# One core of a hybrid decoder step: the sample's attention steps stand still while the prompt's attention outputs are merged

## The chip, the cores and the metric

The kernel runs on one core of a Trainium2 chip. The metric is the device time of one launch in microseconds (us): the median of three runs before the change is 1683.92 us (1680.46 to 1686.54). TensorE is called PE, VectorE DVE, ScalarE ACT, GpSimd POOL, and SyncE, which issues most transfers, SP.

## The reference, cut to what matters

One layer of a decoder for 1024 prompt tokens and 32 sample tokens (8 sequences of 4). All arithmetic is float32.

```
h = rmsnorm(x) * (1 + sc1) + sh1
q, k, v, u_lin, u_gate, gate_a, gate_b = split(h @ w_in)
a = conv_tail(depthwise(u_lin * sigmoid(u_gate))) @ w_conv_out
for three groups of 4 heads (windows 128, 512, 2048, dilations 1, 4, 16):
    prompt: o, lse = dilated attention over the group's own keys
    sample: o, lse = attention over the cached keys and values and the 4 new ones
o = sum over groups of softmax(lse over groups) * o        # the merge
b = o @ w_attn_out
x = x + g1 * ((sigmoid(gate_a) * a + sigmoid(gate_b) * b) @ w_out)
x = x + g2 * moe(rmsnorm(x) ...)     # top 2 of 32 experts, then the outputs
```

## The kernel before

The order of the work is written out by hand: each engine has one queue, and instructions stand in it in the order in which the program emits them. An engine that waits for one instruction holds up all that stand behind it.

**Pieces.** The product `h @ w_in` is made in pieces of 128 columns (`run_piece`, line 1089; list `pieces`). There are 50: for each of six head pairs q, k and v (and for the first four pairs two pieces of the convolution's input, ul and ug), numbers 0 to 25; then the gates, ga c and gb c, and from the third pair of gates on a piece ab c that multiplies the convolution's and the attention's outputs by w_conv_out and w_attn_out. So 26 to 31 are ga0, gb0, ga1, gb1, ga2, gb2; 32 is ab0; 33 and 34 are ga3 and gb3; 35 is ab1; then ga4, gb4, ab2, ga5, gb5, ab3 and so on to 49. A piece has three column parts of 352 tokens. Numbers are split into a high and a low part, so that each product is three matmuls: a gate piece has 3 x 8 x 3 = 72 of them, an ab piece 3 x (12 + 6) = 54. A gate piece is evacuated by ACT (tanh, line 1141), out of three PSUM buffers; an ab piece by DVE (lines 1114 to 1121). The weights of the next piece are split while a piece runs: the high part by ACT (line 171), the low part (line 172) by POOL for pieces up to 33 and by DVE from 34 on.

**Modulation.** From piece 34 on, two units of the second modulation product run in each piece (`run_mb`, line 1060): a load of 512 KB, a split by ACT and DVE (tiles mbh, mbl), four matmuls.

**Ticks.** Everything else is written as generators that are advanced a step at a time by `tick()` (line 1183). A piece has 9 ticks, the first one 3, so that piece j holds ticks 9j - 5 to 9j + 3. One tick advances the attention generators (`att_bg`) by one step; the convolution (`conv_bg`) in two ticks of three; and the low-priority generators (`low_bg`) in two ticks of three, those whose number leaves 0 or 2 when divided by 3.

**The merge.** `att_bg` runs the prompt's attention of the six head pairs and then `merge_gen` (line 861). Each of eight row blocks is loaded from a DRAM buffer (og, line 869) that the attention wrote; DVE and, for one exponential, ACT (line 834) merge the groups (`merge_steps`, lines 824 to 854), two blocks at a time; PE transposes the result (line 895), ACT and DVE split it into oTh and oTl (lines 898, 900), and the block two pairs later is loaded. The generator starts at tick 247. It has 42 steps and would end at tick 288, but piece 31 ends with tick 282, and ahead of piece 32 (ab0), the first reader of oTh and oTl, the program drains `att_bg` (line 1261): the last six steps are emitted there with no ticks between them.

**The sample's attention.** `low_bg` runs `sample_logits` for each head group and then `sample_out` (line 970): a first step (the new rows' output, the first load, the maximum and the exponentials), which falls on tick 246; a second with three products of the new values (tile pt_vx, line 984), on tick 248; then 20 chunks of cached values, two steps each. A chunk is four loads of 128 KB by SP (line 927, issued one chunk ahead), one multiply by POOL over 128 x 1024 elements (line 999), one reduction (line 1001) and one addition (line 1002) by DVE. Chunk k (1 to 20) is reduced at tick 249 + 3k. Behind the chunks come a trip through DRAM, a small merge and one transpose, step 56 being the last, at tick 329 (piece 37).

All large tiles come from one pool of 44 slots. A load into a slot waits for the last reader of what the slot held.

Behind the pieces come the product with w_out and the router (`p4_mm` and its neighbours), then the experts, whose weights are streamed from HBM, then the outputs.

Of the kernel before, what the change touches and what calls it, by code (L numbers as in the profile page):

```python
# [72 lines left out]
def nrow(i):  # L73
    return NS if i == SI else P
# [66 lines left out]
def hybrid(ctx, tc, A, O):  # L141
# [12 lines left out]
    def slot(shape, name, dtype=F32):  # L154
        return slots.tile(shape, dtype, name=name, tag="s", bufs=NSLOT)
# [4 lines left out]
    def ptr(shape, name):  # L160
        return ps.tile(shape, F32, name=name, tag="T", bufs=2)
# [4 lines left out]
    def f(ap):  # L166
        return ap.bitcast(F32)
# [319 lines left out]
    def mm3(out, wpair, ks, xs, cols, tick=None):  # L487

        hi, lo = wpair
        n = len(ks)  # L490
        for a, (k, (xh, xl)) in enumerate(zip(ks, xs)):
            pe.matmul(out, hi[:, k], xh[:, cols], start=a == 0, stop=False)  # L492
            pe.matmul(out, lo[:, k], xh[:, cols], start=False, stop=False)  # L493
            pe.matmul(out, hi[:, k], xl[:, cols], start=False, stop=a == n - 1)  # L494
            if tick and a in (2, 5):
                tick()
# [25 lines left out]
    conv_bg, att_bg, low_bg = Bg(), Bg(), Bg()  # L522
# [301 lines left out]
    def merge_steps(n, nparts, src, o):  # L824

        v = src.rearrange("p (g h) x -> p g h x", h=4)
        nm = ep.tile([P, 4], F32, name="mg_nm", tag="mg_nm", bufs=2)
        dve.tensor_reduce(nm[:n], v[:, :, :, 64].rearrange("p g h -> p h g"), axis=AX.X, op=ALU.min)
        yield
        w = ep.tile([P, 4, 4], F32, name="mg_w", tag="mg_w", bufs=2)  # L830
        wv = w[:n, 0:nparts]
        dve.tensor_tensor(wv, nm[:n, None, :].to_broadcast([n, nparts, 4]), v[:, :, :, 64], op=ALU.subtract)
        yield
        act.activation(wv, wv, AF.Exp)
        yield
        ws = ep.tile([P, 4, 4], F32, name="mg_ws", tag="mg_ws", bufs=2)
        dve.tensor_tensor(ws[:n, 0:nparts], wv, v[:, :, :, 65], op=ALU.mult)
        yield
        den = ep.tile([P, 4], F32, name="mg_d", tag="mg_d", bufs=2)
        dve.tensor_reduce(den[:n], ws[:n, 0:nparts].rearrange("p g h -> p h g"), axis=AX.X, op=ALU.add)  # L840
        yield
        dve.reciprocal(den[:n], den[:n])
        yield
        dve.tensor_tensor(wv, wv, den[:n, None, :].to_broadcast([n, nparts, 4]), op=ALU.mult)
        yield
        o = o.rearrange("p (h d) -> p h d", h=4)
        tm = v[:, :, :, 0:64]
        dve.tensor_tensor(tm, tm, wv[:, :, :, None].to_broadcast([n, nparts, 4, HD]), op=ALU.mult)
        yield
        dve.tensor_tensor(o[:n], tm[:, 0], tm[:, 1], op=ALU.add)  # L850
        yield
        for gg in range(2, nparts):
            dve.tensor_tensor(o[:n], o[:n], tm[:, gg], op=ALU.add)
            yield
# [6 lines left out]
    def merge_gen():  # L861
        for c in range(2):
            oT.append((slot([P, S], f"oTh{c}", F32R), slot([P, S], f"oTl{c}", F32R)))
        tt, o = {}, {}

        def load(i):
            if i < 8:
                tt[i] = slot([P, SLOT], f"mg{i}")
                sp.dma_start(tt[i][:, 0:792], og[i * P:(i + 1) * P].rearrange("p a x -> p (a x)"))

        load(0)
        load(1)
        for _ in range(8):
            yield
        for i in range(0, 10, 2):
            ms = []
            for k in (i, i + 1):
                if k < 8:
                    t = tt[k]
                    ms.append(merge_steps(P, 3, t[:, 0:792].rearrange("p (a x) -> p a x", x=66), t[:, 792:1048]))  # L880
            for _ in zip(*ms):
                pass
            if not i:
                load(2)
                load(3)
            yield
            yield
            yield
            yield
            for k in (i - 2, i - 1):  # L890
                if k >= 0:
                    q = tt.pop(k)[:, 792:1048]
                    pt = ptr([P, 2, P], f"pt_o{k}")
                    for c in range(2):
                        pe.transpose(pt[:, c], q[:, c * P:(c + 1) * P], ident)
                    cs = slice(k * P, (k + 1) * P)
                    for c in range(2):
                        act.activation(oT[c][0][:, cs], pt[:, c], AF.Copy)
                    for c in range(2):
                        dve.tensor_tensor(oT[c][1][:, cs], pt[:, c], f(oT[c][0][:, cs]), op=ALU.subtract)  # L900
                    load(k + 4)
                    yield
            yield


    oTs = cp.tile([P, 2, NS], F32, name="oTs")
# [113 lines left out]
    def copy_gen():  # L1020
        for g in range(3):
            keep = (124, 508, 1024)[g]
            drop = CACHE[g] - keep
            n = keep * 512
            m = n // (1, 2, 4)[g]
            for b in range(DB):
                for o in range(0, n, m):
                    sp.dma_start(dap(kvs[g], b * (keep + 4) * 512 + o, [[m // 16, 16], [1, m // 16]]),
                                  dap(caches[g], (b * CACHE[g] + drop) * 512 + o, [[m // 16, 16], [1, m // 16]]))
                    yield  # L1030
        sp.dma_start(conv_s[0, :, 0:26].rearrange("b r c -> b (r c)"),
                       A["state_conv"][0, :, 4:30].rearrange("b r c -> b (r c)"))
        yield
# [55 lines left out]
    def run_piece(j):  # L1089
# [19 lines left out]
        for n in range(3):  # L1109
# [20 lines left out]
            else:  # L1130
                if j == 0:
                    pm = pms[n]
                else:
                    pm = pmm([P, NTILE], f"pm_{j}_{n}")
                    mm3(pm, W[j], range(KC), hT, cs, tick)
# [25 lines left out]
            for _ in range(3 if kind == "ab" else 1):  # L1161
                tick()
        W[j] = None
        if kind == "ul":
            lin[c] = dst
        elif kind == "ug":
            lin.pop(c)
            conv_bg.add(conv_gen(c))
            if c == 3:
                conv_bg.add(conv_tail())  # L1170
        elif kind in ("q", "k", "v"):
            qk.setdefault(c, {})[kind] = dst
            if kind == "v":
                att_bg.add(pair_gen(c))
                if c == 5:
                    att_bg.add(merge_gen())
# [1 line left out]
    setup = [dw_T, state_T] + [lambda p=p: bias_rows(p) for p in range(6)] + [early_t.clear]  # L1178
    copies, wo_bg = Bg(), Bg()
    copies.add(copy_gen())  # L1180
    state = {"n": 0}

    def tick():
        n = state["n"] = state["n"] + 1
        if n % 3 == 0:
            if setup:
                setup.pop(0)()
            if n > 45:
                copies.step(1, 1)
        att_bg.step(1, 1)  # L1190
        if n % 3 or CR:
            conv_bg.step(1, 1)
        if n % 3 != 1:
            low_bg.step(1, 1)
            wo_bg.step(1, 1)

    for j in range(2):
# [626 lines left out]
    with tc.If(vmax > P + HB):  # L1824
# [25 lines left out]
        for i in range(9):  # L1850
            n = nrow(i)
# [151 lines left out]
```

## Time and profile before

| | us |
|---|---|
| median of three runs | 1683.92 |
| profiled execution, its own time | 1680.3 |
| span of the profiled execution | 1678.5 |
| mean granted PE clock over the span | 0.956 |
| pieces 26 to 31, from the sample's second step (579.65) to ab0 (651.62) | 72.0 |
| ab0 (651.62) to the start of ga3 (664.69) | 13.1 |
| ga3 to the start of ab1 (689.95) | 25.3 |
| ab1 to the start of ga5 (743.02) | 53.1 |

Times within the span are counted from its first instruction. The stretches by piece begin at the piece's first matmul on PE. A row of windows gives for each engine the time in which it was busy and the number of its instructions, then the granted clock of PE (1.00 is full speed), the share of the DMA engines and GB/s. In a row of a group of instructions the mean duration of one and its number are what is wanted; in a row of waits the total, the number of times and the longest.

### The profile page before, as it was taken

Reading aid. Unit: us, or ns where it says so; the run is one execution under the profiler, and the core shown is the slowest. Engines: PE = TensorE matmul, PEld = TensorE weight load, DVE = VectorE, ACT = ScalarE, POOL = GpSimd, SP = SyncE. Lnnn points to the kernel's source line nnn. Section 1 sums busy time; section 2 is a strip of 40 time slices with the busy share of each in tenths; the row PEclk is TensorE's granted clock in tenths of the full one; section 3 lists DMA queues with packets and bytes.
Section 4 is the critical chain, followed back from the end, with each engine's and each line's share of the span. In section 5 each row is a group of like instructions: output and inputs, shape, how many; then the busy total and the mean of one; then the engine's idle time right before and its main releaser. Section 6 shows DMA issues by size and latency. Waiting matters only on the chain. (4 is left out here: it accounts for less than half of the span.)

```text
span 1678.5 us, 22927 instructions
## 1 busy us (share of the span) xinstructions
PE 1523.2 (91%) x8238; PEld 1067.2 (64%) x8238; DVE 868.1 (52%) x1502; ACT 457.8 (27%) x938; POOL 466.0 (28%) x403
## 2 busy tenths in 40 slices
PE   5999989999799887999989996999999999999991
PEld 3789978998789776899977875433333333333330
DVE  5684878777933689844465466222222222222224
ACT  7523332333244411233333321111111111111113
POOL 2111143113411454300003434222242333332330
PEclk9899998999999988999999996799999999999996
DMA  9132365354442564744467329878799999999996
GB/s 327 53 108 84 133 191 189 104 187 124 140 121 63 135 169 127 201 134 149 128 226 220 126 72 361 312 237 310 259 383 387 397 382 386 373 394 387 383 345 218
DMA packets 202030, 378.73 MB, mean 226 GB/s; under 512 B 33981, under 2 KB 121193, under 8 KB 200976
## 3 DMA queue, kind: packets, MB, share of 16 engines
q1 hardware_dynamic: 183095, 346.79, 59.0%
q0 software_dynamic: 18784, 29.99, 6.8%
q8 instruction: 88, 1.44, 0.3%
q14 instruction: 63, 0.51, 0.1%
HBM read 358.00 MB, written 66.93 MB: 253 GB/s over the span
## 5 line engine op out<-in xcount | busy, mean ns | idle before, releaser
L492 PE MATMUL pm<-hTh,wh 128*128 128x352 f32 x984 | 340.7, 346 | 3.0 <-ACT wh L171 3.0
L493 PE MATMUL pm<-hTh,wl 128*128 128x352 f32 x984 | 324.8, 330 | 8.3 <-POOL wl L172 8.3
L494 PE MATMUL pm<-hTl,wh 128*128 128x352 f32 x984 | 323.3, 329 | 0.0
L1675 PE MATMUL gu<-raw,x0s 128*64 128x512 f32 x1024 | 237.9, 602 | 14.0 <-PEq L1803 4.8
L492 PEld LDWEIGHTS pm<-hTh,wh 128*128 128x128 f32 x984 | 190.1, 193 | 15.3 <-issue 4.4
L493 PEld LDWEIGHTS pm<-hTh,wl 128*128 128x128 f32 x984 | 190.5, 194 | 13.0 <-POOL wl L172 11.6
L172 POOL TENSOR_TENSOR wl<-wr,wh 128x1024 fp32r<-128x1024 f32 (+1 forms) x34 | 84.4, 2482 | 381.5 <-ACT wh L171 286.1
L494 PEld LDWEIGHTS pm<-hTl,wh 128*128 128x128 f32 x984 | 190.2, 193 | 0.0
L1675 PE MATMUL py<-raw,xhs 128*64 128x512 f32 x768 | 174.0, 592 | 0.5 <-ACT xhs L1696 0.5
L1675 PEld LDWEIGHTS gu<-raw,x0s 128*64 128x64 f32 x1024 | 74.9, 137 | 151.3 <-issue 141.4
L557 DVE SCALAR_TENSOR_TENSOR acc<-u,dwT,acc 128x1024 f32<-128x1024 f32 x120 | 169.8, 1415 | 0.0
L1690 DVE SCALAR_TENSOR_TENSOR hu<-hu,gu 64x512 f32<-64x512 f32 x48 | 32.6, 679 | 257.6 <-ACT hu L1689 122.4
L1675 PEld LDWEIGHTS py<-raw,xhs 128*64 128x64 f32 x768 | 56.4, 137 | 108.7 <-issue 104.5
L1660 POOL DMA_INDIRECT x2d<-yts,ixd x32 | 51.7, 1616 | 255.0 <-DVE wxc L1714 238.5
L1675 PE MATMUL gu<-raw,xhs 128*64 128x512 f32 x512 | 113.4, 595 | 2.1
L1655 POOL DMA_INDIRECT xe<-h2d,ix x96 | 98.8, 1029 | 37.7 <-issue 27.5
L1688 ACT ACTIVATE hu<-gu 64x512 f32<-64x512 f32 x48 | 28.4, 592 | 213.2 <-PE gu L1675 210.0
L1669 DVE COPY x0s<-pX 128x256 f32<-128x256 f32 x32 | 13.6, 424 | 140.3 <-ACT xhs L1696 71.7
L1675 PEld LDWEIGHTS gu<-raw,xhs 128*64 128x64 f32 x512 | 35.3, 137 | 68.3 <-issue 64.5
L1696 ACT ACTIVATE xhs<-pH 128x256 f32<-128x256 f32 x48 | 18.4, 384 | 208.2 <-PE pH L1695 155.0
L172 DVE TENSOR_TENSOR mbl<-mbw,mbh 128x1024 fp32r<-128x1024 f32 x32 | 40.9, 1277 | 54.6 <-ACT mbh L171 54.5
L761 ACT ACTIVATE Sb<-Sb,stage 128x128 f32<-128x128 f32 (+1 forms) x96 | 42.3, 442 | 93.9 <-DVE stage L758 44.8
(411 smaller groups left out, 2495.4 us busy)
## 6 DMA issues: line engine op xcount, KB each, us to landing
raw<-in_w_exp_gate_dram SPq DMA_DIRECT2D x128, 512.0 KB
raw<-in_w_exp_up_dram SPq DMA_DIRECT2D x128, 512.0 KB
raw<-in_w_exp_down_dram SPq DMA_DIRECT2D x128, 512.0 KB
wr<-in_w_in_dram SPq DMA_DIRECT2D x42, 512.0 KB
kv<-in_cache_kv_w_dram SPq DMA_DIRECT2D x160, 128.0 KB
out_dram<-in_cache_kv_w_dram SPq DMA_DIRECT2D x32, 512.0 KB
mbw<-in_w_mod_dram SPq DMA_DIRECT2D x32, 512.0 KB
x<-in_x_prompt_dram SPq DMA_DIRECT2D x16, 512.0 KB
```

The lines of the kernel that those rows point to most:

```text
L172: sub.tensor_tensor(lo, raw, f(hi), op=ALU.subtract)
L492: pe.matmul(out, hi[:, k], xh[:, cols], start=a == 0, stop=False)
L493: pe.matmul(out, lo[:, k], xh[:, cols], start=False, stop=False)
L494: pe.matmul(out, hi[:, k], xl[:, cols], start=False, stop=a == n - 1)
L557: dve.scalar_tensor_tensor(acc[:, 0:S], u[:, j:j + S], w, acc[:, 0:S], op0=ALU.mult, op1=ALU.add)
L761: act.activation(Sb[:, c0:c1], Sb[:, c0:c1], AF.Exp, bias=stage[:, blk[a], hh, 64:65], accum_out=stage[:, blk[a], hh, 65:66])
L1655: pool.indirect_dma_start(out=xe[b][:, i % 2], out_offset=None, in_=h2h, in_offset=bass.IndirectOffsetOnAxis(ap=ix, axis=0), bounds_check= ...
L1660: pool.indirect_dma_start(out=x2h, out_offset=bass.IndirectOffsetOnAxis(ap=ix, axis=0), in_=buf, in_offset=None, bounds_check=2 * NT - 1, ...
L1675: pe.matmul(out[r], x, w[h], start=start, stop=stop, tile_position=(0, h * HB))
L1688: act.activation(h, GU[0:HB], AF.Tanh, scale=0.5)
L1690: dve.scalar_tensor_tensor(h, h, 1.0, GU[0:HB], op0=ALU.add, op1=ALU.mult)
L1696: act.activation(hT_, pH[:, 0:256].rearrange("p (c x) -> p c x", c=2), AF.Copy)
```

## The change

A flag `hold` is set when `merge_gen` starts and cleared when it ends. While it is set, `tick()` doesn't advance `low_bg`. The generator `wo_bg` goes on as before.

```diff
@@ merge_gen
+        state["hold"] = True
         load(0)
         load(1)
         for _ in range(8):
...
                     load(k + 4)
                     yield
             yield
+        state["hold"] = False
@@
-    state = {"n": 0}
+    state = {"n": 0, "hold": False}
@@ tick
         if n % 3 != 1:
-            low_bg.step(1, 1)
+            if not state["hold"]:
+                low_bg.step(1, 1)
             wo_bg.step(1, 1)
```

`merge_gen` starts in tick 247 and ends in the drain behind tick 282. The ticks 247 to 282 hold 24 steps of `low_bg`; these and all later ones of `sample_out` move by 36 ticks, or four pieces. Its first step, on tick 246, stays where it was. The second moves from tick 248 to tick 284, at the beginning of piece 32. Chunk k is reduced at tick 285 + 3k instead of 249 + 3k: before, 11 chunks fell on ticks up to 282, three each on pieces 32, 33 and 34; after, two fall on piece 32 and three each on pieces 33 to 38. The last step moves from tick 329 to tick 365, in piece 41. No instruction is added or left out.

## Rows read from the trace of the kernel before

**Rows 1.** The page's span in 40 equal slices of 42 us: busy tenths of PE, granted clock of PE, busy tenths of the DMA engines.

```profile
PE   5999989999799887999989996999999999999991
...
PEclk9899998999999988999999996799999999999996
DMA  9132365354442564744467329878799999999996
```

**Rows 2.** Windows: busy time and instructions of PE, PEld, DVE, ACT and POOL in each stretch, PE clock, DMA share, GB/s. The stretches are: pieces 26 to 29, from the sample's second step on; pieces 30 and 31; ab0; ga3; gb3; ab1; ga4; gb4; ab2; ga5; gb5.

```profile
581.55:602.19 20.64, 20.64 (x127) 20.37 (x127) 15.56 (x26) 3.01 (x7) 9.04 (x5) 1.00 1.06 249
602.19:651.62 49.43, 31.84 (x162) 29.86 (x160) 48.53 (x81) 8.89 (x30) 22.53 (x10) 0.81 0.41 112
651.62:664.69 13.07, 11.11 (x56) 10.85 (x55) 12.77 (x17) 1.89 (x5) 8.56 (x4) 0.82 0.63 148
664.69:676.30 11.61, 11.61 (x74) 11.61 (x73) 10.26 (x11) 1.88 (x3) 3.72 (x2) 1.00 0.73 220
676.30:689.95 13.65, 13.64 (x83) 12.42 (x81) 9.22 (x7) 4.30 (x7) 5.86 (x4) 1.00 0.81 192
689.95:705.22 15.27, 11.27 (x62) 9.65 (x63) 15.10 (x17) 4.03 (x5) 4.52 (x4) 1.00 0.52 152
705.22:719.04 13.82, 13.82 (x84) 12.63 (x82) 9.46 (x19) 4.49 (x8) 1.05 (x2) 1.00 0.62 191
719.04:732.57 13.53, 13.53 (x83) 12.68 (x82) 3.41 (x3) 3.80 (x8) 0.22 (x1) 1.00 0.34 114
732.57:743.02 10.45, 10.45 (x63) 9.59 (x62) 8.17 (x13) 3.56 (x4) 0.82 (x2) 1.00 0.46 135
743.02:756.46 13.44, 13.44 (x82) 12.57 (x80) 4.54 (x6) 3.87 (x7) 0.52 (x1) 1.00 0.57 173
756.46:769.87 13.41, 13.41 (x82) 12.54 (x80) 4.76 (x5) 4.02 (x7) 0.52 (x1) 1.00 0.37 112
```

**Rows 3.** Waits of PE from 581.5 to 651.7: who waited for whom, us in total, times, longest.

```profile
PE pt_o L895 <- DVE oTl L900: 10.3, 2, 7.9
PE pm L493 <- POOL wl L172: 4.3, 2, 2.2
PE pm L492 <- ACT wh L171: 3.0, 2, 2.5
```

**Rows 4.** Waits of ACT from 575 to 740, in the same columns.

```profile
ACT mg_w L834 <- DVE mg_w L832: 34.8, 4, 15.5
```

**Rows 5.** Waits of SP from 560 to 740, in the same columns; L869 loads the merge's blocks, L927 the sample's chunks.

```profile
SPq L869 <- DVE so_t L1001: 18.2, 3, 7.5
SPq L927 <- DVE so_t L1001: 10.8, 3, 6.5
```

**Rows 6.** Groups of DVE's instructions in pieces 30 and 31 (602.19 to 651.62): busy us, mean ns of one.

```profile
L1001 DVE TENSOR_REDUCE so_t<-kv 128x256 f32<-128x1024 f32 x8 | 15.6, 1949 | 0.2
L850 DVE TENSOR_TENSOR mg<-mg 128x256 f32<-128x256 f32 x6 | 10.8, 1841 | 0.0
L848 DVE TENSOR_TENSOR mg<-mg,mg_w 128x768 f32<-128x768 f32 x6 | 9.8, 1671 | 0.0
L853 DVE TENSOR_TENSOR mg<-mg 128x256 f32<-128x256 f32 x6 | 5.7, 995 | 0.0
```

**Rows 7.** The tile mg over the whole span: shortest, median and longest ns of the three large instructions of the merge.

```profile
L848 DVE TENSOR_TENSOR mg<-mg,mg_w x8: 951/959/3100, 594.9 to 642.5; 128x768 f32<-128x768 f32 x8
L850 DVE TENSOR_TENSOR mg<-mg x8: 412/2086/2154, 596.7 to 645.3; 128x256 f32<-128x256 f32 x8
L853 DVE TENSOR_TENSOR mg<-mg x8: 411/417/2162, 597.3 to 647.7; 128x256 f32<-128x256 f32 x8
```

**Rows 8.** Timeline of 602 to 616: start, duration, engine; the merge of blocks 2 and 3 on DVE beside POOL.

```profile
604.45 3.97 DVE L848 TENSOR_TENSOR mg<-mg,mg_w 128x768 f32<-128x768 f32 x2
...
605.11 2.49 POOL L172 TENSOR_TENSOR wl<-wr,wh 128x1024 fp32r<-128x1024 f32 x1 [5.21 <-issue]
...
607.57 6.81 POOL L999 TENSOR_TENSOR kv<-kv,LB 128x1024 f32<-128x1024 f32 x3
...
608.34 4.23 DVE L850 TENSOR_TENSOR mg<-mg 128x256 f32<-128x256 f32 x2
```

**Rows 9.** The sample's own instructions by line, over the whole span: shortest, median and longest ns.

```profile
L984 PE MATMUL pt_vx<-kvn,selt x6: 374/374/479, 579.6 to 581.3; 32*128 32x256 f32 x6
...
L999 POOL TENSOR_TENSOR kv<-kv,LB x20: 1922/2034/2651, 580.2 to 694.3; 128x1024 f32<-128x1024 f32 x20
...
L1001 DVE TENSOR_REDUCE so_t<-kv x20: 1870/1990/2033, 583.5 to 697.5; 128x256 f32<-128x1024 f32 x20
...
L1002 DVE TENSOR_TENSOR so<-so,so_t x20: 425/426/2014, 585.6 to 699.5; 128x256 f32<-128x256 f32 x20
```

**Rows 10.** The low half of the modulation's split by DVE: first over the whole span (shortest, median, longest ns), then groups of DVE's instructions in ab1, ga4 and gb4 (689.95 to 732.57; busy us, mean ns).

```profile
L172 DVE TENSOR_TENSOR mbl<-mbw,mbh x20: 1208/1226/2958, 678.0 to 799.3; 128x1024 fp32r<-128x1024 f32 x20
...
L172 DVE TENSOR_TENSOR mbl<-mbw,mbh 128x1024 fp32r<-128x1024 f32 x6 | 9.1, 1510 | 6.7 <-ACT mbh L171 6.7
...
L1002 DVE TENSOR_TENSOR so<-so,so_t 128x256 f32<-128x256 f32 x3 | 2.3, 765 | 0.1
```

**Rows 11.** Timeline of DVE: the last instruction of the last chunk.

```profile
699.50 0.43 DVE L1002 TENSOR_TENSOR so<-so,so_t 128x256 f32<-128x256 f32 x1
```

**Rows 12.** Windows again, of a stretch of later pieces (from gb6 to ab5, 43 to 47), in the columns of rows 2.

```profile
800.00:850.00 50.00, 50.00 (x299) 46.37 (x298) 24.24 (x32) 15.12 (x20) 3.10 (x6) 1.00 0.48 139
```

## The prediction

> **What bounds the kernel now.** I read four views in this order. The page's slices first: PE is nine tenths busy or more through most of the span, with a visible dip in slices 14 to 16, where its clock falls too; from slice 24 on the DMA engines are full as well [rows 1]. Then windows cut at the pieces [rows 2]: pieces 26 to 29 and most pieces from ga4 on keep PE busy all the time, but pieces 30 and 31 take 49.43 us of which PE works 31.84 at a clock of 0.81, while DVE works 48.53. ab0 and ab1 are also longer than PE needs: 13.07 and 15.27 against 10.45 for ab2, which has the same work as ab1 and no sample step. So in this part DVE sets the pace, and PE elsewhere. Later stretches have PE busy for 50.00 of 50 us [rows 12]: time that PE wins here reaches the end, since the router and the stream of expert weights start behind it.
>
> Then the waits. In pieces 26 to 31 PE stands 10.3 us for oTl of DVE, 4.3 for the low half of a weight and 3.0 for the high half [rows 3]. These are three ends of one thing. The exponential of the merge stands in ACT's queue ahead of the gates' evacuation and the weights' high half, and ACT waits 34.8 us in four waits for DVE's instruction in front of it [rows 4]. SP's loads of merge blocks wait 18.2 us for reductions of the sample's chunks that still read the slot [rows 5].
>
> Last, what DVE does there [rows 6]. Eight chunk reductions take 15.6 us. The merge's own instructions are stretched: the 768-wide product has a mean of 1.67 us against a shortest of 0.95, the first addition 1.84 against 0.41, the second 0.995 against 0.41 [rows 6, 7]. The timeline shows with what: two products take 3.97 us while POOL splits a weight, two additions 4.23 us while POOL multiplies three chunks in a row [rows 8]. The stretching costs 6 x (0.72 + 1.43 + 0.58) = 16.4 us.
>
> **Part 1, pieces 26 to 31 without the sample.** For PE, pieces 30 and 31 are 144 matmuls and 16 transposes. At the 20.64 us per 127 instructions of the undisturbed stretch, 0.1625 each [rows 2], the matmuls are 23.4 us; the transposes hide most of their length in the stream, some 1.1 us by my estimate. That is 24.5 against 49.43: 24.9 us at most to be won. Does DVE let it? Of its 48.53 us there, 15.6 are reductions, 8 x 0.43 = 3.4 additions of the sample [rows 9] and 16.4 stretch; 13.1 are left for the merge itself with the oTl splits. POOL's remaining weight splits can each stretch it by their own length, 2.49 [rows 8], three times, which makes 20.6 us at most. That fits into 24.5, and no chunk stands in front of a merge any more. The merge's loads no longer wait for a chunk's reader [rows 5]. I leave 2 us of stall (bounds 0 and 5): won 22.9.
>
> The second step of the sample, 6 matmuls with DVE work between them, leaves this part: PE is kept from 579.6 to 581.55 by it [rows 2, 9], 1.9 us won. It goes to ab0, with the first two chunks. There PE needs the 10.45 of ab2 less its two modulation units (ga5 shows their price: 13.44 - 72 x 0.1625 = 1.7 [rows 2]), plus those 1.9: 10.6. DVE today works 12.77 of 13.07 there [rows 2], and by my estimate some 5 of it are chunks left over from the merge; after, it starts level, with one chunk less and the second step more. PE also no longer arrives there cold (clock 0.82 [rows 2]). I take 12.0 instead of 13.07, bounds 10.6 and 14: 1.1 won. Part 1 together: 22.9 + 1.9 + 1.1 = 25.9 us, bounds 21 and 29.
>
> **Part 2, pieces 33 and 34.** Three chunks each as before, with the same neighbours: 0, bounds -1 and +2. This is also why their rows are the best guide to part 3: gb3 has three chunks and two modulation units and takes 13.65, against 13.44 for ga5 with none [rows 2]. But DVE leaves it late: the last chunk ends at 699.93 [rows 11], 10 us into ab1.
>
> **Part 3, pieces 35 to 38 (ab1, ga4, gb4, ab2) with twelve chunks more.** This is the price. Without sample work DVE needs 8.17, 4.54, 4.76 and 8.17 in such pieces (ab2, ga5, gb5, ab2 of today [rows 2]): 25.6. A chunk adds 1.99 + 0.43 [rows 9] and a gap, 2.45; twelve make 29.4. Stretching by POOL's multiply comes on top. Bounds: 0, and the whole length of the multiply, 2.03 [rows 9]. The nearest rows are those of ab1 to gb4, with three chunks: six splits of the modulation have a mean of 1.51 against a median of 1.23, three additions 0.765 against 0.43 [rows 9, 10], so (6 x 0.28 + 3 x 0.34) / 3 = 0.9 us per chunk; twelve make 10.9. DVE needs 65.9 us where today the four pieces take 15.27 + 13.82 + 13.53 + 10.45 = 53.07. DVE enters 10 us late as today and may leave ab2 up to some 8 us late, since what is then left (two chunks, one evacuation, one split) is needed by nobody at once. So PE loses 65.9 - 53.07 + 10 - 8 = 14.8. What PE can bridge in the two gate pieces may give back a little, and DVE's idle time for late loads can add: I take 14, bounds 5 (DVE's stretch nil, the backlog eaten) and 27 (full stretch). The stop falls on PE's products pa and pb, which wait for DVE's evacuations, and on the modulation and weight splits queued behind a chunk.
>
> What else moves: SP issues 48 of the chunk loads four pieces later, among the loads of modulation and of weights. The trace has that mixture in gb3, and PE was not held there [rows 2]: 0, and its upper price is a rival below. The sample's merge and its DRAM trip move to ga5, gb5 and ab3, where DVE is busy 4.54 of 13.44 [rows 2]: 0.
>
> At one place a rule speaks against the change. The row: the first addition of the merge, 0.41 alone, has a median of 2.09 [rows 7]. The Trainium skill, "SBUF — State Buffer", section "Who interferes with whom", has it that a VectorE instruction with two SBUF inputs and a GpSimd instruction that reads SBUF exclude each other for a whole instruction, and that whichever comes second is blocked. The trace agrees in these durations; so the change would move the lock to the splits and additions behind the hold, not remove it, and with a full block for each multiply the sum would be that of the third case below.
>
> **The sum.** 25.9 - 14 = 11.9 us won. Against the profiled execution's own 1680.3 that is 1668; it lies 3.6 below the median of 1683.92, and for the median the sum gives 1672.0. The bounds, 21 - 27 and 29 - 5, are -6 and +24.
>
> **The rivals.** A measurement of this kernel tells about 0.3%, 5 us, from no change.
> 1. The forecast: 7 to 18 us won. For it: DVE is full in pieces 30 and 31 and has 9 to 10 us idle in each gate piece from gb4 on [rows 2].
> 2. The chunks hide nearly whole behind gates: gb3 carried three at a loss of 0.2 [rows 2]. Only the two ab pieces lose, some 3 us each: 25.9 - 6 = 20 won, 1664. Against: ab1 lost 4.8 with only a backlog.
> 3. Full blocking: each of the twelve multiplies stretches DVE by 2.03, 13.6 us more than taken. 25.9 - 27.6 = 1.7 lost, 1686; within 0.3%. Against: the reductions, the chunk's longest part, keep to 1.87 to 2.03 throughout [rows 9], so much of a multiply falls on work that it doesn't stretch.
> 4. The merge keeps PE waiting by its own chain of load, DVE, ACT, PE: each of three pairs holds ACT by some 4 us. Part 1 falls by 12 to about 14, and the time stays at 1684. Against: in pieces 26 to 29 the first pair costs PE nothing [rows 2].
> 5. Slower: SP's queue sets the pace of pieces 35 to 38. Each chunk's loads wait for a slot, 3.6 us by the mean of three waits [rows 5], and the modulation's and weights' loads stand behind them; twelve times is 43 us. If 40% reaches PE, 17 us, the sum is 25.9 - 14 - 17 = 5 lost: 1689. It decides from 28% (12 us) on. Against: gb3 again.
> 6. The hold does nothing measurable, because the flag covers too few steps: 24 of 56 are covered by the count of ticks, so this would need the count to be wrong; 1684.
>
> **How the numbers follow.** Chances: 1, 0.58; 2, 0.14; 3, 0.09; 4, 0.09; 5, 0.07; 6, 0.03. Faster by over 0.3%: the first and the second, 0.72. Within 0.3%: cases 4 and 6 and most of 3, 0.19. Slower by over 0.3%: case 5 and the rest of 3, 0.09. Prediction 1672, the likeliest case. The range leaves out the best of case 2 and the worst of 3 and 5: 1661 to 1685.
>
> **What would show each step.** Part 1: pieces 30 and 31 in 25 to 29 us, DVE under 90% busy there, no wait of ACT's exponential over 3 us, oTl gone from PE's waits, the clock near 1.00; the first addition of the merge near 0.41 unless a weight split runs. Part 3: the last reduction of a chunk at the end of ab2, the two ab pieces at 15 to 18 us each with PE waiting for evacuations (L1114, L1121) or splits (L172), the gate pieces near 14. The prediction is wrong if the merge's stretch still takes 35 us or more, if ab1 to ab2 together exceed 75 us, or if they stay under 58.

## The result, and the profile after

The changed kernel takes 1693.21 us (median of 14 runs, 1685.86 to 1697.63) against 1681.47 us for the kernel before (14 runs, 1676.86 to 1686.54): a ratio of 1.0059 with a 95% interval of 1.0045 to 1.0073. That is 11.7 us slower by the medians and 9.9 by the ratio, which does not go by the medians. The forecast was 1672 with a range of 1661 to 1685. The profiled execution's own time is 1693.3, its span 1691.5, its mean PE clock 0.952.

Where the time went is read from the starts of pieces on PE. Line numbers behind the merge's start are one or two higher than in the kernel before, and a few more in experiments that add lines. Each kernel was profiled twice; one execution of each beside the other of the same kernel shows which differences belong to the change. All in us:

| stretch | before | after | before, again | after, again |
|---|---|---|---|---|
| start to a point 24 matmuls ahead of the sample's second step of before | 575.6 | 572.1 | 571.0 | 575.1 |
| from there to piece 30 | 26.6 | 24.5 | 26.6 | 24.5 |
| pieces 30 and 31 | 49.4 | 24.9 | 48.4 | 24.9 |
| ab0 | 13.1 | 11.6 | 13.1 | 13.1 |
| ga3, gb3 | 25.2 | 25.8 | 25.3 | 25.2 |
| pieces 35 to 38 (ab1, ga4, gb4, ab2) | 53.1 | 85.6 | 54.1 | 86.7 |
| ga5 to the first matmul of the product with w_out | 143.2 | 146.6 | 142.5 | 146.4 |
| product with w_out and router, to the experts | 175.5 | 181.9 | 176.8 | 176.8 |
| experts and outputs | 616.8 | 618.4 | 616.8 | 617.1 |
| span | 1678.5 | 1691.5 | 1674.6 | 1689.8 |

Up to the end of ab0, 28.1 us were won in the first pair and 25.6 in the second. From ga3 to the product with w_out 36.5 and 36.4 were lost. The first stretch lies ahead of the change and differs by 4 us in either direction; the product with w_out was 6.4 longer in one profile and not in the other.

Windows of the changed kernel, in the columns of [rows 2]; the stretches are those of the table's second to fourth row, then ga3 with gb3, ab1, ga4, gb4, ab2, ga5 with gb5:

```profile
572.12:596.65 24.53, 24.53 (x152) 24.23 (x152) 13.26 (x41) 6.70 (x20) 5.94 (x4) 1.00 0.47 133
596.65:621.60 24.95, 24.95 (x162) 24.82 (x160) 12.09 (x48) 7.50 (x25) 4.42 (x3) 1.00 0.32 103
621.60:633.16 11.56, 10.61 (x63) 9.60 (x62) 9.54 (x16) 1.93 (x6) 8.61 (x4) 1.00 0.51 136
633.16:658.97 25.81, 25.41 (x154) 23.90 (x152) 19.90 (x18) 6.17 (x10) 7.94 (x4) 1.00 0.74 180
658.97:678.50 19.53, 13.50 (x62) 11.08 (x63) 15.59 (x18) 3.47 (x4) 7.33 (x4) 0.88 0.77 186
678.50:700.10 21.60, 15.45 (x82) 13.12 (x80) 13.56 (x14) 4.56 (x7) 7.00 (x6) 0.90 0.69 178
700.10:718.88 18.78, 16.00 (x82) 14.32 (x80) 15.12 (x12) 3.72 (x6) 5.82 (x3) 0.80 0.44 130
718.88:744.64 25.76, 13.43 (x62) 11.37 (x62) 16.97 (x18) 3.41 (x5) 7.77 (x5) 0.73 0.57 141
744.64:774.70 30.06, 27.79 (x162) 25.21 (x162) 19.52 (x27) 8.96 (x14) 4.13 (x5) 1.00 0.51 150
```

In pieces 30 and 31 PE works all the time at full clock, with DVE busy for 12.09 us instead of 48.53. In pieces 35 to 38 neither engine is full: PE works 58.4 of 85.67 us at a clock of 0.73 to 0.90, DVE 61.2. PE's work there was 49.1 of 53.07 before [rows 2]: of the 32.6 lost, 9.3 are matmuls that run slower after PE has stood, 23.3 are standing.

The tile mg of the changed kernel (shortest, median, longest ns), the answer to [rows 7]:

```profile
L848 DVE TENSOR_TENSOR mg<-mg,mg_w x8: 951/955/960, 586.4 to 615.4; 128x768 f32<-128x768 f32 x8
L850 DVE TENSOR_TENSOR mg<-mg x8: 415/418/420, 588.2 to 616.6; 128x256 f32<-128x256 f32 x8
L853 DVE TENSOR_TENSOR mg<-mg x8: 414/418/421, 588.8 to 617.3; 128x256 f32<-128x256 f32 x8
```

None of these three large instructions is stretched any more: the first addition's median falls from 2.086 to 0.418 us. (One small instruction of the merge, L832, took 1.81 us at 583.29 against a median of 0.18, while POOL split a weight from 582.68 to 585.07.) The rule that the prediction weighed there (the Trainium skill, "SBUF — State Buffer", section "Who interferes with whom": two inputs of DVE and a read of SBUF by POOL exclude each other) agrees with that pair of numbers.

DVE's waits in pieces 35 to 38 of the changed kernel (who for whom, us in total, times, longest):

```profile
DVE mbr L1082 <- DMA mbr<-in_b_mod_dram: 12.4, 2, 7.3
DVE so_t L1003 <- POOL kv L1001: 6.5, 3, 2.8
DVE wl L172 <- ACT wh L171: 5.5, 3, 3.0
DVE mbl L172 <- ACT mbh L171: 1.2, 2, 0.7
```

PE's waits in the same stretch:

```profile
PE pb L492 <- DVE mT L1116: 15.9, 3, 11.4
PE mb L1075 <- DVE mbl L172: 6.4, 4, 5.6
```

DVE's groups there (busy us, mean ns of one, idle us before them):

```profile
L1003 DVE TENSOR_REDUCE so_t<-kv 128x256 f32<-128x1024 f32 x13 | 25.4, 1954 | 6.5 <-POOL kv L1001 6.5
L1004 DVE TENSOR_TENSOR so<-so,so_t 128x256 f32<-128x256 f32 x13 | 12.5, 959 | 0.4
L172 DVE TENSOR_TENSOR mbl<-mbw,mbh 128x1024 fp32r<-128x1024 f32 x8 | 10.9, 1361 | 1.2 <-ACT mbh L171 1.2
L172 DVE TENSOR_TENSOR wl<-wr,wh 128x1024 fp32r<-128x1024 f32 (+1 forms) x5 | 5.6, 1114 | 5.5 <-ACT wh L171 5.5
```

DVE's 61.2 us busy and 25.6 us of waits fill the 85.67 (a wait can overlap the end of the instruction before it, so 24.4 us are really idle). The largest wait is for the bias row of a modulation block, a load of 512 numbers to each of nine partitions, which POOL issues once in four units. POOL's instructions (start, duration, instruction, idle before it and its releaser):

```profile
683.42 0.59 POOL L1081 DMA_DIRECT2D mbr<-in_b_mod_dram  x1 [8.43 <-DVE sbs L1125]
...
722.21 2.92 POOL L1001 TENSOR_TENSOR kv<-kv,LB 128x1024 f32<-128x1024 f32 x1 [9.81 <-DMA kv<-in_cache_kv_w_dram]
725.07 0.56 POOL L1081 DMA_DIRECT2D mbr<-in_b_mod_dram  x1
732.30 0.52 POOL L1088 DMA_DIRECT2D modd<-mbr  x1 [6.67 <-DVE mbr L1083]
732.84 3.83 POOL L1001 TENSOR_TENSOR kv<-kv,LB 128x1024 f32<-128x1024 f32 x2
```

and DVE's around them:

```profile
682.95 0.17 DVE L1125 COPY sbs<-gb 128x32 f32<-128x32 f32 x1
683.04 1.22 DVE L172 TENSOR_TENSOR mbl<-mbw,mbh 128x1024 fp32r<-128x1024 f32 x1
689.35 0.68 DVE L1082 TENSOR_TENSOR mbr<-mbr,mb 9x512 f32<-9x512 f32 x1 [5.10 <-DMA mbr<-in_b_mod_dram]
...
722.11 1.22 DVE L172 TENSOR_TENSOR mbl<-mbw,mbh 128x1024 fp32r<-128x1024 f32 x1
730.62 0.67 DVE L1082 TENSOR_TENSOR mbr<-mbr,mb 9x512 f32<-9x512 f32 x1 [7.30 <-DMA mbr<-in_b_mod_dram]
...
733.86 3.10 DVE L1004 TENSOR_TENSOR so<-so,so_t 128x256 f32<-128x256 f32 x1
```

By the releasers that the profile infers, the first load waits for a slot that DVE frees late (its copy at 682.95), and DVE then stands 5.10 us for it. The second stands behind a chunk's multiply, which itself waited 9.81 us for the chunk's load; DVE stands 7.30. The two loads, 18 KB each, are also long on their way: 5.6 us from issue to landing, the median of the two. In the kernel before, the first such load was issued at 705.6 and the addition that waits for it began at 708.5, 2.9 us later. So of DVE's 7.30 us only 1.8 lie ahead of the load's issue; issued earlier, it would have been on its way before DVE came to it, which number 1 below tries. Then the store of the block (L1088) holds the next two multiplies until 732.84, and these stretch DVE's addition to 3.10. PE's longest wait, 11.4 us for the evacuation L1116, is the end of this chain. Before the change the chunks are over at 699.9 [rows 11], ahead of the first block.

### The profile page after: what moved, and what is told of

Its sections match the earlier page's. It is cut to its first block, busy times and chain, and to the rows that moved or that the text cites. A ratio compares the mean times of both kernels' runs of the same rounds, so it can differ in the third digit from the quotient of the medians.

```text
span 1691.5 us, 22920 instructions
## 1 busy us (share of the span) xinstructions
PE 1528.4 (90%) x8238; PEld 1067.7 (63%) x8238; DVE 858.0 (51%) x1502; ACT 457.9 (27%) x938; POOL 464.7 (27%) x403
## 5 line engine op out<-in xcount | busy, mean ns | idle before, releaser
L493 PEld LDWEIGHTS pm<-hTh,wl 128*128 128x128 f32 x984 | 190.0, 193 | 14.1 <-POOL wl L172 6.8
L492 PEld LDWEIGHTS pm<-hTh,wh 128*128 128x128 f32 x984 | 189.9, 193 | 12.4 <-issue 4.5
L1693 DVE SCALAR_TENSOR_TENSOR hu<-hu,gu 64x512 f32<-64x512 f32 x48 | 32.6, 679 | 257.6 <-ACT hu L1692 122.4
```

Source lines behind the costliest of these rows:

```text
L1693: dve.scalar_tensor_tensor(h, h, 1.0, GU[0:HB], op0=ALU.add, op1=ALU.mult)
```

## The experiments

The theories, by the letters that the texts use. A: DVE stands in its queue for transfers that are issued late, above all the bias row of a modulation block. B: POOL's multiplies stretch DVE's splits and additions by more than was taken. C: time is lost behind the pieces, by a lower clock. D: SP's queue and the slots, with 48 chunk loads among those of weights and modulation. E, formed after the first runs: a chunk holds up DVE's queue, and with it PE, by nearly its own length wherever it stands, so moving chunks doesn't pay; the late bias adds to that. Ratios are to the kernel before, measured beside each version, with the 95% interval; its medians were 1682.86 (first four), 1683.56 (next four), 1682.49 (next four) and 1680.61 us (last two).

**1. The changed kernel with the bias row loaded early.** POOL loads it at the first unit of the block instead of the last, into two small tiles of their own; nothing else differs.

```diff
+mb["b"] = [ep.tile([NS, 256], F32, name=f"mbb{cb}{a}", tag="qn", bufs=2) for a in range(2)]
+for a in range(2):
+    bsrc = A["b_mod"][0, 2 * D + cb * 512 + a * 256:2 * D + cb * 512 + (a + 1) * 256]
+    pool.dma_start(mb["b"][a][0:9], dap(bsrc, 0, [[0, 9], [1, 256]]))
...
-pool.dma_start(t[:, 0], dap(bsrc, 0, [[0, 9], [1, 512]]))
-dve.tensor_tensor(t[:, 0], t[:, 0], pm[0:9], op=ALU.add)
+for a, b in enumerate(mb.pop("b")):
+    dve.tensor_tensor(t[:, 0, a * 256:(a + 1) * 256], b[0:9], pm[0:9, a * 256:(a + 1) * 256], op=ALU.add)
```

> The changed kernel with one thing different: the bias row of a modulation block (18 KB, issued by POOL) is loaded into a small buffer at the block's first unit instead of its fourth, so that it neither stands behind a chunk's multiply that waits for its data nor waits for a large slot. Theory A (DVE stands still in its queue for transfers issued late): DVE's waits at the bias addition (12.4 us in two in pieces 35 to 38 of the changed kernel) fall under 3, pieces 35 to 38 (ab1 to ab2) go from 85.7 to 73 to 79 us, and the time falls by 6 to 13 us against the changed kernel. Theory B (the loss is DVE's work stretched by POOL's multiplies): no change beyond 3 us. Theory C (the loss beyond the forecast lies behind the pieces, in a lower clock): no change in the end time beyond 3 us.

Measured: 1679.36 us, 0.9985 (0.9968 to 1.0003). Window of this kernel's pieces 35 to 38:

```profile
666.10:738.70 72.60, 55.14 (x284) 47.56 (x284) 59.73 (x59) 14.91 (x20) 29.68 (x19) 0.93 0.75 187
```

and its longest wait of PE there:

```profile
PE pb L492 <- DVE mT L1119: 8.9, 4, 3.6
```

The stretch falls from 85.67 to 72.6 us, the longest wait for an evacuation from 11.4 to 3.6; A had expected a stretch of 73 to 79. A small load issued late was worth 13.8 us by the medians and 12.4 by the ratios, more than the whole loss either way; A holds, though what is left is still 19.5 above 53.1. The edit takes the load out of its place in the queue and out of the shared slots, and gives its long way time to pass; the three weren't tried apart.

**2. The changed kernel without most chunk loads.** Two chunk tiles are used again and again, 72 of the 80 loads of values are left out; all arithmetic stays.

```diff
-pend.append(load_chunk(*order[n + 1], 1))
+pend.append(load_chunk(*order[n + 1], 1) if n == 0 else prev)
```

> The changed kernel without the loads of the sample's value chunks from the third on: the first two tiles are used again and again, so that POOL and DVE do the same work on them; 72 of 80 loads of 128 KB are left out. Theory A: the multiplies no longer wait for transfers (47.2 us in eight waits before), SP's queue and the slots are free for the modulation's loads; pieces 35 to 38 fall to 62 to 70 us, DVE's own 61 being the floor; the time falls by 14 to 24 us against the changed kernel. Theory B: the multiplies still stretch DVE's additions and splits, the pieces stay above 78 us, the time falls by under 6. Theory C: under 3.

Measured: 1681.67, 0.9999 (0.9982 to 1.0015). Window of its pieces 35 to 38, and DVE's wait for the bias there, 6.5 us instead of 12.4:

```profile
658.40:735.50 77.10, 56.50 (x286) 48.43 (x284) 63.15 (x57) 14.83 (x19) 27.26 (x16) 0.87 0.29 89
...
DVE mbr L1083 <- DMA mbr<-in_b_mod_dram: 6.5, 2, 4.1
```

Every theory missed: A had 62 to 70 us for these pieces, B over 78. With the arithmetic in place the loads are worth 8.6 us of the stretch, and 24.0 of the 32.6 lost remain without them. Number 9 shows that the loads by themselves cost next to nothing. What they do in the trace of the changed kernel is hold POOL's multiply (9.81 us ahead of the one at 722.21), and the bias load behind it.

**3. The changed kernel without POOL's multiply of the values** (line 1001 of the changed kernel left out, 20 times).

> The changed kernel without POOL's multiply of the value chunks; loads, reductions and additions stay. Theory B: DVE's additions of the sample go back from a mean of 0.96 us to 0.43, 9 to 10 us of DVE time are won in pieces 35 to 38, which fall from 85.7 to about 74, and the rest of the loss stays. Theory A: POOL's queue no longer holds the bias load (one of its two waits goes, 5 to 7 us), but the reductions now wait for the loads themselves: pieces 35 to 38 at 72 to 80. The two differ in what DVE waits for: by A DVE still stands 10 us or more for transfers, by B under 5.

Measured: 1669.07, 0.9928 (0.9901 to 0.9955). Window of its pieces 35 to 38:

```profile
663.00:725.90 62.90, 53.92 (x286) 47.38 (x285) 51.84 (x57) 14.85 (x19) 2.13 (x4) 0.92 0.77 201
```

and the group of the sample's additions there:

```profile
L1003 DVE TENSOR_TENSOR so<-so,so_t 128x256 f32<-128x256 f32 x12 | 5.1, 426 | 0.4
```

Without the multiply DVE is busy for 51.8 instead of 61.2. Some 0.8 of these 9.4 us is one addition and the end of a reduction that the changed kernel's window has more, so the stretch is about 9 us in sum, 13 x (0.959 - 0.426) = 6.9 of it in the additions. The prediction had 10.9, so B is refuted as a reason for the miss. The multiply costs 24.1 us in all by the medians, with what stands behind it: the pieces fell to 62.9 us, below what both A (72 to 80) and B (about 74) had expected. The gains of numbers 1, 2 and 3 in these pieces, 13.1, 8.6 and 22.8, add up to more than the 32.6 lost, so they overlap.

**4 and 5. A slower pace behind the hold**: one tick of three instead of two; number 5 with the early bias as well.

```diff
-        state["hold"] = False
+        state["hold"], state["slow"] = False, True
...
-            if not state["hold"]:
+            if not state["hold"] and not (state["slow"] and n % 3):
```

> The changed kernel with the sample's steps, once released, advanced in one tick of three instead of two: one chunk in six ticks, so that the twenty chunks are spread over pieces 32 to 46. DVE's work per gate piece is then 4.6 + 1.5 chunks of 2.45, 8 to 9 us of 13.4, per ab piece 12 of 10.5. Theories A and B alike: the gain of the merge (30 us by the start of ab0) is kept but for 1 to 3 us per ab piece; the time falls by 20 to 30 us against the changed kernel, to 1660 to 1670. Theory C: the time stays within 8 us of the changed kernel's.

> Slow pace as before (one chunk in six ticks behind the hold) together with the early bias load. Theory A' (what the slow pace cost is the bias block: POOL's bias load waits for a slot or a multiply, DVE waits for the bias, the chunks' multiplies wait for the store of the block, and the slow pace lets four such blocks meet chunk steps instead of two): without the late bias load the ab pieces behind a block (22.3 and 23.6 us at slow pace) fall to 11 to 14, and the time comes to 1660 to 1670, below both the kernel before and the changed one with the early bias. Theory D (slots: every piece in which chunk tiles live costs time, since loads wait for slots): the time stays above 1685, and the pieces with chunks still lose 3 us or more each.

Measured: 1705.13, 1.0132 (1.0105 to 1.0159), and with the early bias 1691.01, 1.0046 (1.0029 to 1.0063). Windows of ab2 and ab4 without the early bias:

```profile
709.00:731.30 22.30, 13.21 (x63) 11.46 (x62) 12.45 (x13) 3.40 (x4) 4.90 (x4) 0.77 0.41 120
...
805.90:829.50 23.60, 13.95 (x64) 12.22 (x63) 13.16 (x15) 3.37 (x4) 5.40 (x5) 0.78 0.40 114
```

and with it:

```profile
704.20:718.10 13.90, 11.24 (x64) 9.48 (x63) 12.48 (x15) 3.41 (x4) 6.10 (x5) 1.00 0.71 188
...
791.50:813.90 22.40, 12.78 (x63) 11.04 (x63) 14.22 (x16) 3.36 (x4) 5.92 (x6) 0.77 0.41 119
```

A slower pace spreads the chunks over more pieces, and so over more modulation blocks: DVE waits for the bias six times, 25.6 us in sum. ab2 falls to 13.9 with the early load; ab4 stays long, for there the block has a second load (L1086 in the changed kernel, of norm_ffn_g) which the edit left late, and for which DVE stands 4.5 us. The price of the bias recurs, 14.1 us. Numbers 4 and 5 missed the 1660 to 1670 that A and B gave them by 35 and 21 us, and number 5 came out where D had it, above 1685: fewer chunks per piece don't make a chunk cheaper. That is where E comes from.

**6. The early bias, and no sample step in ab pieces behind the hold** (`not (state["slow"] and state["ab"])` in tick()), so that PE's waits for evacuations should go.

> The early bias load, and behind the hold the sample's steps at the old pace, but in gate pieces alone, none in ab pieces, where DVE has least room. Theory A': ab pieces at 10.5 to 12, gate pairs at 27 to 29 against 26.9; time 1658 to 1668. Theory D: chunk tiles live until piece 43, so the time is above 1680.

Measured: 1682.18, 0.999 (0.9973 to 1.0007), no faster than number 1. Window of its ab2:

```profile
708.80:728.20 19.40, 14.52 (x63) 12.24 (x63) 17.28 (x18) 3.37 (x4) 7.68 (x6) 0.82 0.61 163
```

The expectation by A', 1658 to 1668, is missed by 14 us; D's, above 1680, is met. ab2 takes 19.4 us though no step is advanced in it: DVE (busy for 17.28) brings the backlog of the gate pieces along.

**7 and 8. The kernel before with the early bias, and the kernel before once more for a second profile.**

> The kernel before with the early bias load alone. Theory A': the sample's steps are over when the first block ends there, so the bias load costs nothing: within 3 us of the kernel before. If it gains 8 us or more, the early load helps by itself, and its gain in the changed kernel says nothing of the hold.

> The kernel before, profiled once more. In the changed kernel and in three of its variants the clock falls to 0.56 to 0.76 for some microseconds in the product with w_out (around 950 to 975 us), where the first profile of the kernel before shows 1.00, and the stretch from its first matmul to the experts' first takes 178 to 183 us against 175.5. If that dip varies from execution to execution, this profile may have it too; if it hangs on the changed order, this profile has none and takes 175 to 176 us.

Measured: 1681.44, 0.9992 (0.9976 to 1.0008), and 1676.35 in one run. Before the change the early load is worth nothing that can be measured: no chunk is left when the first block ends. The second profile is the third column of the table above; its product with w_out took 176.8 us, 1.3 more than in the first.

**9. The changed kernel with the chunk loads alone**: multiply, reduction and addition of the values are left out.

> The changed kernel with the chunks' loads alone: POOL's multiply, DVE's reduction and addition of all twenty value chunks are left out, the 80 loads and their slots stay. Theory D (the loads, SP's queue and the slots that the chunk tiles take cost the time): pieces 35 to 38 stay above 62 us (85.7 with everything, 62.9 without the multiply). Theory E (DVE's queue: a chunk costs PE nearly its own length on DVE wherever it stands, since PE runs only a few buffers ahead of DVE): pieces 35 to 38 come to 48 to 52 us, 47.8 being PE's own work, and the time to 1650 to 1660.

Measured: 1656.83, 0.9836 (0.9817 to 0.9856). Windows of its ab1, ga4 with gb4, and ab2 together:

```profile
661.60:715.90 54.30, 49.85 (x286) 44.11 (x285) 24.05 (x33) 15.12 (x20) 2.72 (x5) 1.00 0.97 231
```

With every load in its place in SP's queue, and the DMA engines at 0.97, the four pieces take 54.3 us against 53.1. So the loads and SP's queue by themselves do not cost the time, and that half of D is refuted. Its other half, the slots, is not fully tested: a chunk tile that nothing reads comes free as soon as its load has landed, and SP's waits ahead of chunk loads (L929, from 621 to 750) sum to 24 us here against 31 in the changed kernel. The price of the chunks comes with their arithmetic and what that holds up: by the medians less 1656.83, 36.4 us in the changed kernel, 22.5 with the early bias (number 1), 25.7 in the kernel before.

**10. Half the pace through the merge instead of the hold, with the early bias.** By E the price should fall if DVE's free time on both sides is used.

```diff
-            if not state["hold"]:
+            if not state["hold"] or n % 3 == 0:
                 low_bg.step(1, 1)
```

> Instead of holding the sample's steps during the merge, they go on at half pace (one tick of three), with the early bias load: six chunks in the merge's pieces, five fewer behind them than in the changed kernel. Theory E: a chunk costs about 2 us behind the merge (22.7 us for eleven in the changed kernel with the early bias load), and in the merge 25 us for eleven, so that the price is nearly the same on both sides: time 1672 to 1684. If the merge's price grows faster than its chunks (its last chunks meet a DVE that is already full), the half pace wins: 1665 to 1672.

Measured: 1675.70, 0.9965 (0.995 to 0.998): faster than both kernels. Windows of its pieces 30 and 31, ab0 to gb3, and 35 to 38:

```profile
600.40:630.60 30.20, 25.95 (x163) 24.75 (x161) 29.32 (x59) 7.83 (x27) 14.42 (x7) 1.00 0.51 137
630.60:667.10 36.50, 35.59 (x208) 34.14 (x206) 30.16 (x32) 7.70 (x15) 19.33 (x12) 0.96 0.72 185
667.10:732.30 65.20, 54.73 (x288) 47.69 (x287) 50.95 (x68) 16.46 (x21) 21.49 (x16) 0.92 0.65 173
```

The merge's two pieces pay 5.3 us more than with the hold, pieces 35 to 38 7.4 less than in number 1.

**11 and 12. The kernel before without the multiply, and without reduction and addition, of chunks 1 to 11**, to see what fills DVE in the merge.

> The kernel before without POOL's multiply in chunks 1 to 11, those that fall beside the merge; loads, reductions and additions stay. If the stretch by POOL (16.4 us) is what fills DVE there, pieces 30 and 31 fall from 49.4 us to 28 to 36 and the time to 1660 to 1668; if the reductions' own 19 us are what counts, they stay above 38.

> The kernel before without DVE's reduction and addition in chunks 1 to 11; loads and multiplies stay. DVE loses 19 of its 48.5 us in pieces 30 and 31, the stretch by POOL stays: 27 to 33 us if DVE's sum is what counts, time 1662 to 1668; above 38 if the stretch of the merge alone holds PE.

Measured: 1668.58, 0.9911 (0.9894 to 0.9929), and 1668.65, 0.9911 (0.9884 to 0.9937). Window of pieces 30 and 31 without the multiply:

```profile
602.00:640.00 38.00, 27.55 (x163) 26.46 (x161) 33.22 (x67) 7.80 (x26) 6.99 (x3) 0.89 0.57 150
```

and without reduction and addition:

```profile
600.30:640.80 40.50, 28.41 (x161) 27.34 (x160) 25.88 (x53) 7.62 (x26) 24.18 (x12) 0.87 0.67 160
```

Neither falls to the length named for a single cause (28 to 36, and 27 to 33). Leaving out either half takes away 11.4 and 8.9 of the 24.5 us, the hold all of it: the merge was kept by the stretch and by the length of the reductions in about equal parts, as the prediction's sum had it.

**13. The changed kernel once more**, for a second profile.

> The changed kernel once more, for a second profile of it. E (DVE's queue sets the price of a chunk, the late bias adds to it): pieces 35 to 38 again take 80 to 88 us against 53 before, with 10 to 15 us of DVE waiting for the bias block there, and about 1692 us in all. If the product with w_out comes out near 176 us instead of 181.9, the 5 us there belong to one execution and not to the change, and the single time is near 1687.

Measured: 1691.68 in one run. Pieces 35 to 38 take 86.7 us with 14.1 of waits for the bias. The product with w_out, first in the first profile:

```profile
891.20:1073.10 181.90, 162.80 (x841) 134.04 (x839) 94.30 (x247) 42.78 (x80) 67.72 (x57) 0.85 0.56 199
```

and in the second:

```profile
895.90:1072.70 176.80, 157.22 (x843) 129.39 (x841) 93.95 (x251) 42.79 (x80) 67.84 (x57) 0.88 0.58 204
```

The same instructions at a clock of 0.85 and 0.88: the 5 us are one execution's and not the change's, so C is refuted. The whole time was above the text's 1687, because the part ahead of the change ran 3.0 us later than in the first profile, ab0 took 1.5 and pieces 35 to 38 1.1 more.

**14. Half the pace through the merge, with the bias load left where it was.**

> Instead of the hold the sample's steps go on at one tick of three through the merge, with the bias load of the modulation block where the kernel before has it. E: the pace alone shares the price between both sides and leaves fewer chunks to meet the first modulation block; the late bias of the one block that still meets chunk steps costs 3 to 8 us: 1676 to 1684 us, ratio .997 to 1.001. If the early bias was worth nothing here: 1675.7, ratio .9965. If the early bias carried the whole gain of the version with both: 1684 to 1690.

Measured: 1689.12, 1.0051 (1.0033 to 1.0068). Windows of its pieces 30 and 31, ab0 to gb3, and 35 to 38:

```profile
601.90:632.00 30.10, 25.87 (x163) 24.60 (x161) 29.35 (x59) 7.68 (x26) 14.31 (x7) 1.00 0.52 138
632.00:670.20 38.20, 36.00 (x209) 34.22 (x207) 33.31 (x34) 7.88 (x15) 19.20 (x10) 0.96 0.70 177
670.20:746.90 76.70, 58.26 (x287) 51.01 (x287) 49.66 (x64) 16.01 (x21) 17.83 (x13) 0.84 0.57 147
```

The likeliest outcome by E, 1676 to 1684, was too low: pieces 35 to 38 lose 11.5 us against number 10 with the same chunks, and DVE works 1.3 us less in them. The half pace leaves fewer chunks behind the merge, but the first blocks still meet some, and DVE waits 7.4 us for their bias:

```profile
DVE mbr L1082 <- DMA mbr<-in_b_mod_dram: 7.4, 2, 5.8
```

So the early bias carries the gain of number 10 over the kernel before. What the half pace itself is worth against the hold isn't clear of noise: with the late bias 4.1 us by the medians and 1.3 by the ratios (1.0059 and 1.0051), with the early one 3.7 and 3.4 (0.9985 and 0.9965), and in both pairs the intervals overlap. The four pairs that differ in the bias load alone, by their ratios and a median of 1682: 1.3 us, inside the interval, in the kernel before, 12.4 with the hold, 14.5 with half the pace, 14.5 with the slow pace.

## Why the prediction was wrong

**Part 1 was right.** 25.9 us was forecast, with bounds 21 and 29; 28.1 and 25.6 were measured. Pieces 30 and 31 took 24.95 us, just under the 25 to 29 named as the sign, at full clock, with the three large instructions of the merge at their unstretched length. One sign failed without a price: ACT's exponential was to wait nowhere over 3 us, and its longest wait is 3.5:

```profile
ACT mg_w L834 <- DVE mg_w L832: 3.9, 2, 3.5
```

DVE itself stood there for the load of a merge block (2.75 us up to 612.11). Numbers 11 and 12 show the two causes that the sum rested on. **Part 2**, 0, was 0.6 and -0.1.

**Part 3 failed.** The forecast was 14 lost, bounds 5 and 27; pieces 35 to 38 lost 32.6, and at 85.67 us are past the 75 that the prediction named as the sign of being wrong. The gate pieces, taken at about 14 us, took 21.60 and 18.78, the ab pieces 19.53 and 25.76 instead of 15 to 18. The sum's first step was sound: DVE's need of 65.9 us, with 10 for what it brings along and less 8 for what it leaves, is 67.9; it worked for 61.2, with a stretch of about 9 against 10.9 taken. The two terms held too: the backlog ended 9.4 us into ab1 (668.35), the last chunk 9.2 us into ga5 (753.83). The step that failed is what came out of it: the need was set against the pieces' length as if DVE could work without a gap, and the sentence that DVE's idle time for late loads can add had no price. DVE stood idle for 24.4 us, 12.4 of them waiting for the bias.

The larger part of this miss of 18.6 us, 13.1 in these pieces, is the bias load, which stood under "What else moves" at 0 by omission: that paragraph followed SP's queue and the sample's DRAM trip, and not POOL's queue, onto which the same step puts twelve multiplies. In the rows of before the bias load and the chunks never meet, so the four calm pieces used as the yardstick couldn't show it; the place of the load and the store (L1079 and L1086 in the kernel before) in POOL's queue could be read from the code and the trace, and wasn't.

The rest, 5.5 us (19.5 lost with the early bias instead of 14), is the same term mis-sized: within the bounds, with some of it matmuls at a lower clock (PE is busy for 55.1 us at a mean clock of 0.93 in number 1, for 49.1 at 1.00 before), for which the sum had no term. The sample's end in ga5 and gb5, forecast at 0, cost 3.2 (30.06 against 26.85 in [rows 2]).

**The rivals.** The chunks did not hide behind the gates (case 2): the two gate pieces lost 13.0 us. Full blocking is refuted by the stretch of about 9 us, where twelve times 2.03 would be 24.4. Cases 4 and 6 fall with pieces 30 and 31 at 24.95 us. SP's queue, the case named slower, came nearest in time (1689) by luck: with the loads alone, in the same queue, the stretch is 1.2 us longer than before (number 9). What the forecast lacked as a case is that the price of a chunk is much the same on both sides. For all twenty chunks it is 25.7 us before, and 22.5 where eleven of them are moved and the bias is early: moving all eleven wins 3 us, which isn't clear of noise (number 1, 0.9968 to 1.0003), and the late bias takes 12 to 14. One reading of [rows 1] was off, without weight in the sum: the DMA engines are not full from slice 24 on but work at seven to nine tenths from slice 25 and at nine only from slice 30.

**What is open**: how much of the 13.8 us is the load's place in the queue, how much the slot it waits for and how much its longer way; what the slots cost that chunk tiles keep while their arithmetic is late; and why twelve chunks more cost PE 19.5 us in pieces 35 to 38 of number 1, 1.6 each against 2.45 of DVE's time (E's "nearly its own length" is too much there), though DVE is idle there for a sixth of the time (59.73 of 72.60 busy). That it stands then for POOL (so_t, 4.7 us), ACT (mbl and wl, 2.5 and 1.9) and a chunk's load (1.8) is seen in its waits, but no run took these away.

## What to carry to other kernels

Before steps are moved, list for every queue that they enter what already stands there and who waits for it, small loads first: here a load of one bias row, issued late among the chunks' multiplies, cost more than the change won without it (12 to 14 us against 3). Idle time of an engine that passes work on in order between two others was no free capacity here: price a step on the new side too (1.6 us for PE of 2.45 on DVE, even with the late load removed), and compare it with what it costs on the old one. The fastest version that was tried took the late load off its place and split the work over both sides (number 10, 1675.70 us); the first of the two is the part whose worth is shown.

## What the runs showed of the hardware

A transfer that POOL issues waits for the compute that stands ahead of it in POOL's queue, and this compute for its own data: issued at 725.07 behind a multiply that had waited 9.81 us, it let DVE go on at 730.62. The bias rows were also longer on their way among the chunk loads, 5.6 us from issue to landing, against 2.9 from issue to the addition in the first block of the kernel before. The clock of PE in the product with w_out differed between two executions of the same kernel, 0.85 and 0.88 over 180 us, for 5 us of time: a difference of that size in one profile of each kernel is no finding.
